# An RMS-normalised matrix product: B's first tile and A's second tile come in fp32 by the two hardware queues, and the preparation of A's row blocks is placed anew

## The chip, the core and the metric

The kernel runs on one core of a Trainium2 chip. Its five engines work side by side, each through its own instructions in order: TensorE (PE; PEld is its weight load), VectorE (DVE), ScalarE (ACT), GpSimd (POOL) and SyncE (SP). Three of them also issue DMA transfers: POOL through a software queue that can change the type on the way, SP and ACT through one hardware queue each, which can't. The metric is the device time of one execution in microseconds; for the kernel before it is the median of three runs.

## What is computed

```python
m, k, n = 2048, 2048, 2048            # a, b, gamma in fp32, eps = 1e-5
x = np.matmul(a, b)
rms = np.sqrt(np.mean(x ** 2, axis=-1, keepdims=True) + eps)
return (gamma * x / rms).astype(np.float32)
```

## The kernel before

**Tiles.** A has 16 blocks of 128 rows; K is cut into 16 tiles of 128 (KT), taken in pairs (KP = 8, the loop variable `kp`). B is kept whole in bf16 in `raw[j][kp]`: two halves `j` of 1024 columns, eight pairs of K tiles, two tiles `t` in each. A matmul is 128x128 by 128x512. The eight PSUM banks are `tbank` and `acc[0]` to `acc[6]`. Order is the order of the program text on each engine (`manual_schedule`).

**The head** (blocks 0 to 3 of A, left half of B; lines 450 to 468). A's first pair of K tiles comes in fp32 by the SP and ACT hardware queues into `a0f` (line 106). Everything else comes by POOL's software queue, cast to bf16: in order B pair 0 (two transfers, line 115), A pair 1 (line 119), B pair 1, A pair 2, B pair 2 and so on, with at most eight transfers in flight. PE first runs eight matmuls on zeros (`busy(8)`), then `transpose_first` turns A's first pair (eight fp32 transposes; DVE and ACT copy the result to `head_at`, line 179), then four more on zeros (`busy(4)`). Then for each `kp` `stream` does 14 matmuls into seven banks (line 409), and within them, after the number of matmuls that its last argument gives, `transpose_head(kp + 1)` turns the next pair of A (line 185) through `tbank`, which DVE copies to `head_at` (line 190). `stream_in_parts` does the eighth group in `tbank` (line 438). At `kp` 0 the transposes stand after 12 matmuls.

**The right half of the head** (`stream_right`, lines 476 to 513) streams B's right half as it lands: rows 0 and 1 plainly (four banks), rows 2 and 3 as one step of Strassen's scheme in Winograd's form (seven products of half size instead of eight; `product`, line 361). DVE makes the sums of B's quarters (`b_diff`, `b_rest`) and of A's (`a_sums`).

**Lines 519 to 634** end that scheme for rows 2 and 3 (`product` 6, 3, 5, 4 and `pair_ends`), evict the banks, and ready blocks 4 and 5: ACT's squares give a row norm (`row_norm`), DVE scales the rows to fp16 (`row_factor`, `row_apply`), PE turns them (`transpose_half`, line 198). `first_segment` is the first half-group (blocks 4 and 5, left half).

**Segments** (lines 642 to 763). Groups g = 2 to 7 are pairs of blocks, each with two halves; every half is one segment of Strassen products, and pairs of groups share a second step (`step`, line 400, in `block_segment` and `last_group`). Each later block is loaded by POOL (`load_block`), then `row_norm` on ACT, then `prepare` (line 248): DVE scales it to fp16 in two halves (`a16_half` and the block's own place) and SP turns each half with a DMA transpose (line 253) into `at(mb)`. `finish` (line 309) multiplies finished rows by the inverse root and gamma on DVE and stores them by SP's queue (line 317); an `x` slot is written again only when its store has landed. `last_group` and what follows it is the tail.

Of the kernel before, what the change touches and what calls it, by code (L numbers as in the profile page):

```python
# [17 lines left out]
def kernel(  # L18
# [14 lines left out]
    P = 128  # L33
# [74 lines left out]

    def ah(kp):
        return ah_slot[(kp - 1) % NAH]  # L110

    def load_b(j, kp):
        for t in range(2):
            lo = kp * W2 + t * P
            nc.gpsimd.dma_start(out=raw[j][kp][:, t, :],  # L115
                                in_=b[lo:lo + P, j * HALF:(j + 1) * HALF])

    def load_head(kp):
        nc.gpsimd.dma_start(  # L119
            out=ah(kp),  # L120
            in_=a[0:HB * P, kp * W2:(kp + 1) * W2].rearrange("(r p) k -> p r k", p=P))
        load_b(0, kp)
# [47 lines left out]
    def transpose_first():  # L170
        bank = [tbank, acc[6]]
        view = [b.rearrange("p (r m) -> p r m", r=HB) for b in bank]
        for t in range(2):
            for r in range(HB):
                nc.tensor.matmul(view[t][:, r, :], a0f[:, r, t * P:(t + 1) * P], identity_f,
                                 is_transpose=True, start=(r == 0), stop=(r == HB - 1))
        for t, copy in enumerate((nc.vector.tensor_copy, nc.scalar.copy)):
            for h in range(2):
                copy(out=head_at[:, t, 2 * h:2 * h + 2, :], in_=view[t][:, 2 * h:2 * h + 2, :])

# [67 lines left out]
    def prepare(mb):  # L248
        row_factor(mb)
        src, f = a32.pop(mb), factor.pop(mb)  # L250
        for h, dst in enumerate((a16_half, src.bitcast(FP16)[:, 0:HALF])):
            nc.vector.tensor_scalar_mul(out=dst, in0=src[:, h * HALF:(h + 1) * HALF], scalar1=f)
            nc.sync.dma_start_transpose(at(mb)[:, h * KP:(h + 1) * KP, :], dst)
# [197 lines left out]
    busy(4)  # L451
    for kp in range(KP):
# [7 lines left out]
        stream(kp, before, len(groups1) + {0: 5, 1: 3}.get(kp, 2))  # L460
# [15 lines left out]
    def stream_right(kp):  # L476
# [11 lines left out]
        if kp == KP - 1:  # L488
            product_matmul(PAIR, 1, 7, p7, kp - 1, True)
        product_matmul(PAIR, 1, 2, u4, kp, True)  # L490
# [4 lines left out]

    for kp in range(KP):
# [22 lines left out]
    r2, r3 = HB - 2, HB - 1  # L519
    x11, x12, x21, x22 = (x_chunk(r, c) for r in (r2, r3) for c in (2, 3))  # L520
    copy_on("A")(out=x11, in_=u2)
# [6 lines left out]
    product(PAIR, 1, 6, u2, start=False)  # L528
# [5 lines left out]
    row_apply(HB + 1)  # L534
    evict(plain[2:3], "A")
    product(PAIR, 1, 3, acc[0])
    product(PAIR, 1, 5, u4, start=False)
    turned = [transpose_half(HB, h, (tbank, acc[1])[h]) for h in range(2)]
    take_transposed(HB, 0, turned[0], nc.scalar.copy)
    take_transposed(HB, 1, turned[1], nc.vector.tensor_copy)  # L540
    load_block(HB + 3)
    for r in range(HB):
        take_pre(r)
    square_right(0)
    evict(plain[3:], "A")
    square_right(1)

    def turn(h):
        view = transpose_half(HB + 1, h, (tbank, acc[2])[h])
        take_transposed(HB + 1, h, view, nc.vector.tensor_copy)  # L550

    for kp in range(KP):
        if kp == 6:
            turn(0)
        product_matmul(PAIR, 1, 4, u2, kp, False)
    turn(1)
    load_block(HB + 4)
    a_sums(G0, (3, 1, 2), False)

    def pair_ends():  # L560
        nc.scalar.copy(out=x22, in_=p7)
        nc.scalar.copy(out=x12, in_=u4)
        add(x21, u2, x22)
        add(x22, x12, x22)
        add(x12, acc[0], x12)

# [44 lines left out]
    def first_segment():  # L611
        n, g, j = 0, G0, 0
        nxt = 2 * g + 2
        do(n, 1)
        do(n, 7, False)
        finish(0, (1,))
        pair_ends()
        do(n, 2)
        row_norm(nxt)
        a_sums(g, (4,))  # L620
        finish(0, (0,))
        do(n, 6)
        do(n + 1, 1)
        prepare(nxt)
# [17 lines left out]
    def segment(n):  # L642
# [8 lines left out]
        own = nxt + (g == NG - 2)  # L651
# [7 lines left out]
        if j == 0:  # L659
            square_right(ra - 2)  # L660
            prepare(own)
            a_sums(g, (4,))
            finish(ra - 2, (0, 1) if g < NG - 2 else (0,))
# [19 lines left out]
        if j == 1 and g + 2 < NG:  # L683
            wait_for(at(nxt + 1)[:, KT - 1, 0:1])
            if G0 < g < NG - 3:
# [8 lines left out]
        if j == 0 and g < NG - 2:  # L694
            row_norm(nxt + 1)
        if j == 1:
            a_sums(g + 1, (3,))
            if g == NG - 3:
# [3 lines left out]
        if j == 0 and g == NG - 2:  # L702
# [7 lines left out]
        if j == 0:  # L710
            square_half(rb, 0)
            if g < NG - 2:
# [3 lines left out]
        else:  # L716
            if g == NG - 3:
                prepare(nxt + 2)
# [5 lines left out]
    def block_segment(n):  # L724
# [6 lines left out]
        row_norm(nxt)  # L731
        do(n - 1, 3)
        step(g - 1, 2, W2)
        step(g - 1, 6, X2)
# [3 lines left out]
        prepare(nxt)  # L738
# [9 lines left out]
        row_norm(nxt + 1)  # L748
        add(x10, W2, x10)
        add(x11, W2, x11)  # L750
        take_pre(ra - 2)
        do(n, 7)
        add(x10, X2, x10)
        a_sums(g, (4,))
        prepare(nxt + 1)
# [156 lines left out]
```

## Time and profile before

| | |
|---|---|
| time, median of 3 runs | 219.94 us (218.92 to 220.41) |
| the profiled execution: its time, its span | 218.97 us, 217.2 us |
| mean granted TensorE clock | 0.995 |
| DVE, ACT, POOL busy | 161.4, 113.1, 35.6 us |
| read from HBM, written | 34.60 MB, 16.78 MB |

The span runs from the first to the last instruction; 1.77 us of the execution's time lie outside it. Times in the views are microseconds from the span's start. In a timeline a row is one or more like instructions: start, time taken, engine, line, operation, out<-in, count; square brackets give the idle time before it and what ended it. A matmul's time is modelled with its drain, so neighbours overlap: 128x512 matmuls start 0.216 us apart (16.07 to 19.96, one turn of the head, holds sixteen of them and eight transposes that take 0.45), and the page shows 379 ns for one.

### The profile page before, as it was taken

What the parts mean: (1) busy time and instruction counts of PE and PEld (TensorE: products, weight loads), DVE (VectorE), ACT (ScalarE), POOL (GpSimd) and SP (SyncE); (2) the same over time, 40 slices, a digit from 0 to 9 for tenths busy, and PEclk for the clock granted to TensorE, in tenths of its full rate; (3) what the DMA queues carried; (4) which work ended last, traced back from release to release, by engine and by line L of the source; (5) the groups of instructions that cost most, each with busy time, mean ns of one, the idle gap of its engine ahead of it and who ended that gap; (6) DMA issues with size and microseconds to landing.
All of it is one profiled execution on the core that took longest, in us unless ns stands there. A gap on an engine that the chain in (4) does not pass through costs nothing.

```text
span 217.2 us, 2953 instructions
## 1 busy us (share of the span) xinstructions
PE 207.3 (95%) x1000; PEld 97.2 (45%) x1020; DVE 161.4 (74%) x323; ACT 113.1 (52%) x222; POOL 35.6 (16%) x74
## 2 busy tenths in 40 slices
PE   7999999999999999999999999999999999999960
PEld 3544544444455444444444444444444444444420
DVE  1128869999899997788975899399859883385771
ACT  2110002900599569498626962585777651555771
POOL 7554444334001000100021001102010000000020
PEclk9999999999999999999999999999999999999997
DMA  7999999999959798978674975499985960040455
GB/s 152 168 202 210 201 204 210 212 206 213 405 202 382 290 263 229 330 295 241 162 239 172 340 246 96 187 237 271 278 307 153 284 218 0 0 193 3 193 191 195
DMA packets 37040, 46.60 MB, mean 215 GB/s; under 512 B 22561, under 2 KB 26657, under 8 KB 35745
## 3 DMA queue, kind: packets, MB, share of 16 engines
q0 software_dynamic: 10608, 23.86, 44.8%
q1 hardware_dynamic: 26144, 22.29, 33.9%
q10 hardware_dynamic: 272, 0.26, 0.3%
q8 instruction: 8, 0.13, 0.2%
q14 instruction: 8, 0.06, 0.1%
HBM read 34.60 MB, written 16.78 MB: 237 GB/s over the span
## 4 chain that ended last, share of the span: by engine, by line
PE 68%; DMA 23%; DVE 2%; POOL 2%; issue 2%; ACT 1%; ACTq 0%; DVEq 0%; POOLq 0%
PE acc L361 61%; DMA b<-in_b_dram 18%; DMA early<-in_a_dram 5%; PE acc L400 3%; PE tbank L400 2%; POOL b L115 1%; DVE early L101 1%; PE tbank L361 1%; POOL early L119 1%; ACT a L779 1%; PE acc L198 0%; PE tbank L198 0%; DVE acc L529 0%; DVE x L101 0%; DVE b L101 0%
## 5 line engine op out<-in xcount | busy, mean ns | idle before, releaser
L361 PEld LDWEIGHTS <-s 128*128 128x128 f16 (+1 forms) x312 | 30.5, 98 | 36.9 <-DVE s L338 0.3
L275 ACT ACTIVATE sq<-x 128x1024 bf16<-128x1024 f32 (+1 forms) x33 | 33.2, 1005 | 22.6 <-DVE x L101 18.8
L409 PE MATMUL acc<-b,head_at 128*128 128x512 bf16 x171 | 42.1, 379 | 0.2
L314 DVE SCALAR_TENSOR_TENSOR x<-x,r,gamma_sb 128x1024 f32<-128x1024 f32 x28 | 35.0, 1282 | 0.5
L361 PE MATMUL acc<-b,head_at 128*128 128x512 bf16 x135 | 33.9, 379 | 0.2
L101 DVE TENSOR_TENSOR x<-acc,x 128x512 f32<-128x512 f32 x33 | 22.2, 686 | 12.5 <-PE acc L361 6.7
L361 PEld LDWEIGHTS <-head_at 128*128 128x128 f16 (+1 forms) x192 | 18.7, 98 | 22.2
L361 PE MATMUL acc<-b,at_even 128*128 128x512 bf16 x110 | 26.2, 379 | 0.1
L361 PE MATMUL acc<-early,s 128*128 128x512 bf16 x100 | 25.3, 379 | 0.2
L409 PEld LDWEIGHTS <-head_at 128*128 128x128 bf16 x176 | 16.9, 98 | 19.1
L361 PE MATMUL acc<-b,s 128*128 128x512 bf16 x102 | 24.1, 379 | 0.2
L227 ACT ACTIVATE sq<-a 128x1024 bf16<-128x1024 f32 x22 | 23.3, 1058 | 1.7 <-DMA a<-in_a_dram 1.4
L361 PEld LDWEIGHTS <-at_even 128*128 128x128 f16 x160 | 15.6, 98 | 18.6
L361 PE MATMUL acc<-t_left,s 128*128 128x512 bf16 x93 | 22.2, 379 | 0.1
L115 POOL DMA_DIRECT2D b<-in_b_dram x32 | 17.2, 540 | 20.5 <-DMA b<-in_b_dram 13.8
L448 ACT COPY x<-acc 128x512 f32<-128x512 f32 x7 | 4.0, 581 | 25.3 <-PE acc L409 25.3
L591 ACT COPY acc<-acc 128x512 f32<-128x512 f32 x12 | 6.9, 575 | 10.4 <-PE acc L361 10.4
L190 DVE COPY head_at<-tbank 128x1024 bf16<-128x1024 bf16 x7 | 4.8, 693 | 7.5 <-PE tbank L185 7.5
L296 DVE RECIPROCAL r<-rms 128x1 f32<-128x1 f32 x16 | 2.5, 159 | 9.7 <-ACT rms L291 9.7
L101 DVE TENSOR_TENSOR x<-tbank,x 128x512 f32<-128x512 f32 x9 | 6.2, 690 | 4.2 <-PE tbank L438 4.1
L782 POOL TENSOR_SCALAR x<-x,r 128x512 f32<-128x512 f32 x2 | 1.4, 688 | 47.8 <-DVE r L296 47.8
L593 ACT COPY x<-acc 128x512 f32<-128x512 f32 x10 | 5.8, 584 | 5.3 <-PE acc L361 4.9
(129 smaller groups left out, 243.4 us busy)
## 6 DMA issues: line engine op xcount, KB each, us to landing
out_dram<-x SPq DMA_DIRECT2D x29, 512.0 KB, 3.0
a<-in_a_dram POOLq DMA_DIRECT2D x9, 1024.0 KB, 6.0
b<-in_b_dram POOLq DMA_DIRECT2D x32, 256.0 KB, 9.9
a<-in_a_dram POOLq DMA_DIRECT2D x4, 512.0 KB, 9.8
early<-in_a_dram POOLq DMA_DIRECT2D x7, 256.0 KB, 10.0
gamma_sb<-in_gamma_dram POOLq DMA_DIRECT2D x2, 512.0 KB, 9.8
head_at<-in_a_dram POOLq DMA_DIRECT2D x1, 1024.0 KB, 7.8
out_dram<-x SPq DMA_DIRECT2D x3, 256.0 KB, 2.6
```

What stands on the lines that cost most here:

```text
L101: nc.vector.tensor_tensor(out=out, in0=in0, in1=in1, op=op)
L115: nc.gpsimd.dma_start(out=raw[j][kp][:, t, :], in_=b[lo:lo + P, j * HALF:(j + 1) * HALF])
L190: nc.vector.tensor_copy(out=head_at[:, 2 * kp:2 * kp + 2, :, :], in_=view)
L227: nc.scalar.activation(out=junk, in_=a32[mb][:, h * HALF:(h + 1) * HALF], func=ACTF.Square, scale=2.0 ** -8, accum_out=n2[:, h:h + 1])
L275: nc.scalar.activation(out=sq[:, 0:src.shape[-1]], in_=src, func=ACTF.Square, scale=inv_sqrt_n, accum_out=msq[mb][:, c:c + 1])
L314: nc.vector.scalar_tensor_tensor(out=x, in0=x, scalar=inverse_of[mb], in1=gamma_sb[:, h * HALF:(h + 1) * HALF], op0=ALU.mult, op1=ALU.mult)
L361: nc.tensor.matmul(bank, lhsT[:, kp, :], rhs, start=(start and kp == 0), stop=(kp == KP - 1), skip_group_check=not start)
L400: nc.tensor.matmul(bank, lhsT[:, k, :], rhs, start=(m in (1, 7) and k == 0), stop=(k == KQ - 1), skip_group_check=m not in (1, 7))
L409: nc.tensor.matmul(bank, head_at[:, kt, r, :], head_rhs(c, kt), start=(kt == 0), stop=(kt == KT - 1))
L448: copy_on(engine)(out=x_chunk(*g), in_=banks[g])
L591: nc.scalar.copy(out=b3, in_=b2)
L593: nc.scalar.copy(out=chunks(n)[2], in_=B7)
```

## The change

A's second pair and the first tile of B pair 0 leave POOL's software queue: SP and ACT each issue, behind their half of A's first pair, half of that B tile (into the free slot `x_slot[5]`) and half of A's second pair (into `x_slot[4]`), in fp32. DVE and ACT cast them to bf16 in `transpose_first`. The zero matmuls after it go from four to two, and the transposes of pair 1 come after seven matmuls instead of twelve. In `stream_right`'s last turn four matmuls of product 6 come before product 2 (the copy to `x11` moves with them). Product 4 is done in three parts, with block 4's transposes, the first product of the first segment and block 5's transposes between them; product 7 of that segment comes after its product 2; `pair_ends` adds in another order. In the first segment `prepare` stands ahead of the second `finish`. From g = 3 on blocks 10 to 13 are prepared earlier than before (with the DMA transposes of block 12 held back by `turn=False` until `turn_half`), so that each segment has one block to prepare, with the loads and `finish` calls moved to suit.

```diff
@@ -106,19 +106,28 @@
         queue.dma_start(out=a0f[:, 2 * h:2 * h + 2, :],
                         in_=a[2 * h * P:(2 * h + 2) * P, 0:W2].rearrange("(r p) k -> p r k", p=P))
 
+    b0f = x_slot[HB + 1]
+    for h, queue in enumerate((nc.sync, nc.scalar)):
+        queue.dma_start(out=b0f[:, h * CH:(h + 1) * CH], in_=b[0:P, h * CH:(h + 1) * CH])
+    a1f = x_slot[HB].rearrange("p (r k) -> p r k", r=HB)
+    for h, queue in enumerate((nc.sync, nc.scalar)):
+        queue.dma_start(out=a1f[:, 2 * h:2 * h + 2, :],
+                        in_=a[2 * h * P:(2 * h + 2) * P, W2:2 * W2].rearrange("(r p) k -> p r k", p=P))
+
     def ah(kp):
         return ah_slot[(kp - 1) % NAH]
 
     def load_b(j, kp):
-        for t in range(2):
+        for t in range(1 if (j, kp) == (0, 0) else 0, 2):
             lo = kp * W2 + t * P
             nc.gpsimd.dma_start(out=raw[j][kp][:, t, :],
                                 in_=b[lo:lo + P, j * HALF:(j + 1) * HALF])
 
     def load_head(kp):
-        nc.gpsimd.dma_start(
-            out=ah(kp),
-            in_=a[0:HB * P, kp * W2:(kp + 1) * W2].rearrange("(r p) k -> p r k", p=P))
+        if kp > 1:
+            nc.gpsimd.dma_start(
+                out=ah(kp),
+                in_=a[0:HB * P, kp * W2:(kp + 1) * W2].rearrange("(r p) k -> p r k", p=P))
         load_b(0, kp)
 
     a32 = {}
@@ -174,9 +183,13 @@
             for r in range(HB):
                 nc.tensor.matmul(view[t][:, r, :], a0f[:, r, t * P:(t + 1) * P], identity_f,
                                  is_transpose=True, start=(r == 0), stop=(r == HB - 1))
+        for h, copy in enumerate((nc.vector.tensor_copy, nc.scalar.copy)):
+            copy(out=raw[0][0][:, 0, h * CH:(h + 1) * CH], in_=b0f[:, h * CH:(h + 1) * CH])
         for t, copy in enumerate((nc.vector.tensor_copy, nc.scalar.copy)):
             for h in range(2):
                 copy(out=head_at[:, t, 2 * h:2 * h + 2, :], in_=view[t][:, 2 * h:2 * h + 2, :])
+        nc.vector.tensor_copy(out=ah(1)[:, 0:2, :], in_=a1f[:, 0:2, :])
+        nc.scalar.copy(out=ah(1)[:, 2:4, :], in_=a1f[:, 2:4, :])
 
     def transpose_head(kp):
         view = tbank.bitcast(BF16).rearrange("p (t r m) -> p t r m", t=2, r=HB)
@@ -245,12 +258,19 @@
         a16[mb] = a16_slot[mb]
         nc.vector.tensor_scalar_mul(out=a16[mb], in0=a32.pop(mb), scalar1=factor.pop(mb))
 
-    def prepare(mb):
+    to_turn = {}
+
+    def prepare(mb, turn=True):
         row_factor(mb)
         src, f = a32.pop(mb), factor.pop(mb)
-        for h, dst in enumerate((a16_half, src.bitcast(FP16)[:, 0:HALF])):
+        to_turn[mb] = a16_half, src.bitcast(FP16)[:, 0:HALF]
+        for h, dst in enumerate(to_turn[mb]):
             nc.vector.tensor_scalar_mul(out=dst, in0=src[:, h * HALF:(h + 1) * HALF], scalar1=f)
-            nc.sync.dma_start_transpose(at(mb)[:, h * KP:(h + 1) * KP, :], dst)
+            if turn:
+                turn_half(mb, h)
+
+    def turn_half(mb, h):
+        nc.sync.dma_start_transpose(at(mb)[:, h * KP:(h + 1) * KP, :], to_turn[mb][h])
 
     x_half = {}
     slot_of = {(r, h): r + HB * h for r in range(HB) for h in range(2)}
@@ -448,7 +468,7 @@
             copy_on(engine)(out=x_chunk(*g), in_=banks[g])
 
     transpose_first()
-    busy(4)
+    busy(2)
     for kp in range(KP):
         if kp + 4 < KP:
             load_head(kp + 4)
@@ -457,7 +477,7 @@
         before = [lambda: transpose_head(kp + 1)] if kp + 1 < KP else []
         if kp == KP - 2:
             before.append(lambda: a_sums(PAIR, (3,), False))
-        stream(kp, before, len(groups1) + {0: 5, 1: 3}.get(kp, 2))
+        stream(kp, before, len(groups1) + {0: 0, 1: 3}.get(kp, 2))
         if kp == KP - 1:
             evict(groups1, "ADADADA")
         stream_in_parts(last1, kp)
@@ -486,13 +506,18 @@
         for g, kt in first:
             head_matmul(banks[g], *g, kt)
         if kp == KP - 1:
+            copy_on("A")(out=x11, in_=u2)
             product_matmul(PAIR, 1, 7, p7, kp - 1, True)
+            for k in range(4):
+                product_matmul(PAIR, 1, 6, u2, k, False)
         product_matmul(PAIR, 1, 2, u4, kp, True)
         if kp < KP - 1:
             product_matmul(PAIR, 1, 7, p7, kp - 1, True)
         for g, kt in second:
             head_matmul(banks[g], *g, kt)
 
+    r2, r3 = HB - 2, HB - 1
+    x11, x12, x21, x22 = (x_chunk(r, c) for r in (r2, r3) for c in (2, 3))
     for kp in range(KP):
         load_later(1)
         b_diff(1, kp)
@@ -516,53 +541,50 @@
 
 
 
-    r2, r3 = HB - 2, HB - 1
-    x11, x12, x21, x22 = (x_chunk(r, c) for r in (r2, r3) for c in (2, 3))
-    copy_on("A")(out=x11, in_=u2)
     product_matmul(PAIR, 1, 7, p7, KP - 1, True)
     b_rest(1, KP - 1)
     add(x11, u4, x11)
     evict(plain[:1], "A")
     row_norm(HB)
     row_norm(HB + 1)
-    product(PAIR, 1, 6, u2, start=False)
+    for kp in range(4, KP):
+        product_matmul(PAIR, 1, 6, u2, kp, False)
     nc.vector.tensor_copy(out=u4, in_=u2)
     row_factor(HB)
     row_apply(HB)
     evict(plain[1:2], "D")
     row_factor(HB + 1)
-    row_apply(HB + 1)
     evict(plain[2:3], "A")
     product(PAIR, 1, 3, acc[0])
     product(PAIR, 1, 5, u4, start=False)
+
+    def product_4(lo, hi):
+        for kp in range(lo, hi):
+            product_matmul(PAIR, 1, 4, u2, kp, False)
+
+    product_4(0, 2)
     turned = [transpose_half(HB, h, (tbank, acc[1])[h]) for h in range(2)]
     take_transposed(HB, 0, turned[0], nc.scalar.copy)
     take_transposed(HB, 1, turned[1], nc.vector.tensor_copy)
+    row_apply(HB + 1)
     load_block(HB + 3)
     for r in range(HB):
         take_pre(r)
+    evict(plain[3:], "A")
     square_right(0)
-    evict(plain[3:], "A")
-    square_right(1)
-
-    def turn(h):
-        view = transpose_half(HB + 1, h, (tbank, acc[2])[h])
-        take_transposed(HB + 1, h, view, nc.vector.tensor_copy)
-
-    for kp in range(KP):
-        if kp == 6:
-            turn(0)
-        product_matmul(PAIR, 1, 4, u2, kp, False)
-    turn(1)
-    load_block(HB + 4)
-    a_sums(G0, (3, 1, 2), False)
+    product_4(2, 6)
+
+    def turn_next():
+        for h in range(2):
+            view = transpose_half(HB + 1, h, (tbank, acc[2])[h])
+            take_transposed(HB + 1, h, view, nc.vector.tensor_copy)
 
     def pair_ends():
-        nc.scalar.copy(out=x22, in_=p7)
+        nc.scalar.copy(out=x21, in_=p7)
         nc.scalar.copy(out=x12, in_=u4)
-        add(x21, u2, x22)
-        add(x22, x12, x22)
+        add(x22, x12, x21)
         add(x12, acc[0], x12)
+        add(x21, u2, x21)
 
 
 
@@ -612,16 +634,21 @@
         n, g, j = 0, G0, 0
         nxt = 2 * g + 2
         do(n, 1)
+        square_right(1)
+        turn_next()
+        product_4(6, KP)
+        load_block(HB + 4)
+        a_sums(g, (3, 1, 2), False)
+        do(n, 2)
         do(n, 7, False)
+        pair_ends()
         finish(0, (1,))
-        pair_ends()
-        do(n, 2)
         row_norm(nxt)
         a_sums(g, (4,))
+        prepare(nxt)
         finish(0, (0,))
         do(n, 6)
         do(n + 1, 1)
-        prepare(nxt)
         do(n, 5)
         nc.scalar.copy(out=chunks(n)[2], in_=B7)
         take(n, 22)
@@ -648,7 +675,7 @@
             return
         first = g >= G2 and (g - G2) % 2 == 0
         do(n, 6)
-        own = nxt + (g == NG - 2)
+        own = nxt + (g >= G2)
         if j == 0:
             finish(ra - 1)
             row_norm(own)
@@ -659,8 +686,10 @@
         if j == 0:
             square_right(ra - 2)
             prepare(own)
+            if g == G2 - 1:
+                load_after(at(nxt)[:, KT - 1, 0:1], nxt + 2)
             a_sums(g, (4,))
-            finish(ra - 2, (0, 1) if g < NG - 2 else (0,))
+            finish(ra - 2, (0, 1) if g < G2 else (0,))
         else:
             if not first:
                 square_half(ra, 0)
@@ -682,7 +711,7 @@
         do(n + 1, 1)
         if j == 1 and g + 2 < NG:
             wait_for(at(nxt + 1)[:, KT - 1, 0:1])
-            if G0 < g < NG - 3:
+            if g in (G2,):
                 load_block(nxt + 2)
                 wait_for(a32[nxt + 2][:, 0:1])
             load_block(nxt + 3)
@@ -691,15 +720,15 @@
                 a_two_sums(g)
             a_sums(g + 1, (1, 2))
         do(n, 7)
-        if j == 0 and g < NG - 2:
+        if j == 0 and g < G2:
             row_norm(nxt + 1)
         if j == 1:
             a_sums(g + 1, (3,))
-            if g == NG - 3:
+            if G0 < g < NG - 2:
                 row_norm(nxt + 2)
         do(n, 5)
         take(n, 22)
-        if j == 0 and g == NG - 2:
+        if j == 0 and g >= G2:
             finish(ra - 2, (1,))
         if j == 1:
             take_pre(rb)
@@ -709,13 +738,13 @@
         take(n, 21)
         if j == 0:
             square_half(rb, 0)
-            if g < NG - 2:
+            if g < G2:
                 prepare(nxt + 1)
             if g == G2:
                 b_two(2)
         else:
-            if g == NG - 3:
-                prepare(nxt + 2)
+            if G0 < g < NG - 2:
+                prepare(nxt + 2, g != G2)
             if not first:
                 square_right(rb)
             if g == G0:
@@ -728,14 +757,15 @@
         do(n, 6)
         step(g - 1, 1, X2)
         nc.scalar.copy(out=W2, in_=X2)
-        row_norm(nxt)
+        row_norm(nxt + 1)
         do(n - 1, 3)
         step(g - 1, 2, W2)
+        for h in range(2):
+            turn_half(nxt, h)
         step(g - 1, 6, X2)
         nc.scalar.copy(out=Y2, in_=X2)
         square_right(ra - 1)
         add(x00, W2, x00)
-        prepare(nxt)
         load_after(at(nxt)[:, KT - 1, 0:1], nxt + 2)
         do(n + 1, 1)
         take(n - 1, 12)
@@ -745,14 +775,13 @@
         step(g - 1, 7, W2)
         step(g - 1, 4, X2)
         add(x11, Y2, x11)
-        row_norm(nxt + 1)
         add(x10, W2, x10)
         add(x11, W2, x11)
         take_pre(ra - 2)
+        prepare(nxt + 1)
         do(n, 7)
         add(x10, X2, x10)
         a_sums(g, (4,))
-        prepare(nxt + 1)
         step(g - 1, 3, Y2)
         do(n, 5)
         take(n, 22)
```

## The prediction

> **What bounds the kernel now.** First the page's busy times and slices, for whether one engine decides.
>
> ```profile
> PE 207.3 (95%) x1000; PEld 97.2 (45%) x1020; DVE 161.4 (74%) x323; ACT 113.1 (52%) x222; POOL 35.6 (16%) x74
> ...
> PE   7999999999999999999999999999999999999960
> ```
>
> PE is full from the second slice to the last but one. Next the waits of PE, because a full slice can hide short ones:
>
> ```profile
> PE acc L164 <- DVE pace L155: 1.5, 1, 1.5
> PE tbank L438 <- DVE head_at L190: 0.3, 1, 0.3
> ```
>
> That is the whole list. After 12.01 us PE waits for nobody until its last matmul at 210.2. So whatever the change moves behind the head can only lose time, and a gain must come from the first 12 us or the 7 us behind 210.2, which it leaves as they are. The timeline of PE at the start shows what there is to win:
>
> ```profile
> 4.84 1.06 PE L175 MATMUL tbank<-t_left,early 128*128 128x128 f32 x4
> 5.70 1.06 PE L175 MATMUL acc<-t_left,early 128*128 128x128 f32 x4
> 6.55 1.09 PE L164 MATMUL acc<-sq 128*128 128x512 bf16 x4
> 7.48 2.75 PE L409 MATMUL acc<-b,head_at 128*128 128x512 bf16 x12
> 10.18 0.62 PE L185 MATMUL tbank<-identity,early 128*128 128x128 bf16 x8
> 10.64 0.59 PE L409 MATMUL acc<-b,head_at 128*128 128x512 bf16 x2
> 11.58 0.59 PE L438 MATMUL tbank<-b,head_at 128*128 128x512 bf16 x2 [0.35 <-DVE head_at L190]
> 12.01 2.32 PE L409 MATMUL acc<-b,head_at 128*128 128x512 bf16 x9
> ```
>
> Four zero matmuls from 6.55 take 4 x 0.216 = 0.86 us. From 7.48 the first turn has 16 matmuls and eight transposes, 16 x 0.216 + 0.45 = 3.91 us, but the second begins at 12.01: 0.62 lost, mostly in the 0.94 from 10.64 to 11.58, where two matmuls (0.43) stand before a copy on DVE. The second turn takes 4.06 to 16.07 (0.15 lost, waiting for A's pair 2), the third 3.89. In all 0.86 + 0.62 + 0.15 = 1.63 us.
>
> Last, which transfers feed this. The DMA view of the first issues, and of two stretches by queue (q1 is SP's, q10 ACT's, q0 POOL's):
>
> ```profile
> early<-in_a_dram ACTq DMA_DIRECT2D x1, 256.0 KB, 3.8
> early<-in_a_dram SPq DMA_DIRECT2D x1, 256.0 KB, 3.5
> b<-in_b_dram POOLq DMA_DIRECT2D x1, 256.0 KB, 5.0
> ```
>
> ```profile
> DMA packets 178, 0.17 MB, mean 342 GB/s; under 512 B 11, under 2 KB 178, under 8 KB 178
> ```
>
> ```profile
> q0 software_dynamic: 80, 0.16, 96.5%
> q10 hardware_dynamic: 93, 0.08, 23.0%
> q1 hardware_dynamic: 15, 0.01, 3.2%
> ```
>
> ```profile
> q0 software_dynamic: 112, 0.20, 102.4%
> ```
>
> A's first pair (issued 0.73) lands at about 4.5, B's first tile (issued 1.24) at 6.24. The second fence is 3.0 to 3.5: the hardware queues alone move 0.17 MB in half a microsecond. The third, 3.5 to 4.5, has the software queue beside their last 0.09 MB. The fourth, 5.0 to 7.0, is that queue alone: 0.20 MB in 2 us, against 205 GB/s from 16 us on. POOL's resumed issues tell of the landings after that: A's pair 1 just before 10.42, where POOL's wait on it ends, and from then one transfer every 1.3 us.
>
> **The change part by part.** *Zero matmuls:* two fewer, 0.43, won only where B and `head_at` are ready: PE's earliest first product is 6.55 + 0.43 = 6.98.
>
> *B's tile and A's second pair on the hardware queues.* Behind A's first pair stand 0.52 MB of B and 0.52 MB of A. Their rate has not been seen beside a running software queue, so by rows: from above 0.17 MB in 0.5 us = 0.34 MB/us, from below what the tail got in the third fence, 0.09 MB in about 0.6 us (it was landed by 4.5) = 0.14. I take the middle, 0.24, since in 5 to 7 us the software queue used half of what it moves later and leaves room. From 3.6, with 0.09 MB of A still to move: B at 3.6 + 0.61/0.24 = 6.1, A's second pair 2.2 later at 8.3, each plus 0.4 from the last packet to the landing (as A's first pair shows, 4.1 to 4.54): 6.5 and 8.7. At the ends: 5.8 and 7.3, or 8.4 and 12.1.
>
> *Casts.* Not in the trace from fp32 in SBUF to bf16 at 128x512. DVE's nearest row is line 252, 128x1024 fp32 to fp16 in 0.74 us, so 0.37 to 0.74; half is the nearer, with half the elements. ACT's nearest is line 448, 128x512 in 0.58. On DVE the cast of B stands ahead of the two copies to `head_at` (0.76 for both): whoever waits for B holds them, and all of PE. So the first product is at 6.5 + 0.05 + 0.37 + 0.38 + 0.05 = 7.35, against 7.48. The second matmul needs ACT's half, 6.5 + 0.05 + 0.58 + 0.05 = 7.2: ready. Seven matmuls end at 8.86. The last six transposes need ACT's half of A: 8.7 + 0.05 + 0.58 + 0.05 = 9.4, so they end at 9.4 + 6 x 0.056 = 9.7; seven matmuls to 11.2, two more to 11.65. DVE's copy (0.69, from 9.8 to 10.5) is now beside the seven matmuls, which removes today's stall; what is late next is ACT's cast of A. Second turn at 11.65 instead of 12.01: -0.36. The software queue has two transfers fewer ahead of A's pair 2, so the 0.15 there goes too: -0.51. Best ends: 6.98 + 16 x 0.216 + 0.45 = 10.89, -1.12 - 0.15 = -1.27. Worst: A at 12.1, transposes to 13.1, second turn at 15.05, +3.0 - 0.15 = +2.9.
>
> *The software stream.* A gain at 12 us is kept only if the later tiles come earlier too: POOL waits for a landing every 1.3 us, three a turn, and PE's turn is 3.9; the last tile of B lands at 56.3 (DVE's wait for it ends at 56.38) and PE reads it at 56.72, 0.4 spare. Two transfers fewer are 2 x 1.27 = 2.5 us off the stream; the hardware queues' extra 1.04 MB costs 1.04/0.34 = 3.1 us of the same engines, less what the slack 2 us from 5 to 7 gives, about 1. Sum -0.4, so the stream keeps pace.
>
> The Trainium skill speaks against this: "DMA: Bandwidth & Descriptors", section "Rules for kernel authors", says that spreading transfers over SP, ACT and GpSimd does not help bandwidth, since all run on the same 16 engines and interleave. By the rule alone the stream would end 3.1 - 2.5 = 0.6 later and the gain would be eaten at 56 us; the row of 5 to 7 us is why I do not take it whole.
>
> *stream_right's end:* four matmuls move ahead of product 2, nothing is added, and B's last tile is needed 0.86 later (spare 1.3). The eviction of `acc[0]` and ACT's row norms behind it come 0.86 later: the second norm ends at 63.9 instead of 63.0.
>
> *Lines 519 to 634:* the order on PE changes, not its work. Walking ACT and DVE with their rows: `row_apply(4)` ends 63.4 (transposes at 63.63, covered), ACT's copy of `tbank` 64.4 to 65.4 (1.01), DVE's copy of `acc[1]` 64.8 to 65.5; the first product wants both at 65.4: +0.14. Block 5's transposes end at 68.2, so `a_sums` starts at 69.2 instead of 67.6, and DVE is 1.3 to 1.5 us behind up to 85. The sum s3 is ready at 69.9, needed at 70.3 since product 2 now covers it; today it is 68.3 against 68.43.
>
> *first_segment:* with `prepare` first, the store of `x_slot[0]` stands behind two DMA transposes on SP (1.27 each): issued at 79.4 instead of 75.11, landed 2.6 later at 82.0, where ACT's copy (line 599; 79.08 today) waits with all of ACT behind it. It frees `acc[1]` for the product at 84.1: 1.4 spare. Block 7's second transpose lands 1.2 later at 88.4, its sum s2 is ready at 89.9, needed at 91.0: 1.1 spare. Nothing.
>
> *Blocks 10 to 13 earlier:* ACT's squares of block 10 and 12 (2.6 each) fall into its idle 3.65 before 116.04 and 4.65 before 137.75; DVE's 2.3 for each into 1.60 before 117.55 (0.7 left, pushing a `finish` nobody waits for within 8 us) and 3.63 before 141.15. PE reads block 10 from 128.9, landed 126.7 today and earlier then. POOL's loads get less to wait for. SP's deferred transposes of block 12 follow a product that ends at 141, now 143.5. Nothing.
>
> Sum: -0.51 + 0.14 = -0.4: 218.97 - 0.4 = 218.6 for the profiled execution. Its time is 0.97 under the median of 219.94; the same step from the median gives 219.5.
>
> **The rivals.** *The whole window closes:* rate 0.34, -1.27 + 0.14 = -1.1, 217.8 (median 218.8). For: 342 GB/s and the slack from 5 to 7. Against: three queues then share 16 engines.
>
> *A's second pair comes late (the other side):* PE is in order, so a landing after 8.3 (8.97 less ACT's 0.68) holds the transposes and all behind them one for one; from 9.1 on the change loses. At 0.14 MB/us it is +2.9 + 0.14, 222.0 (median 223.0); at 0.19, A's first pair's own mean (0.52 MB from 1.8 to 4.5), the landing is 10.0, +0.9 in all, 219.9 (median 220.8). It loses over 1% from a landing at 11.3. For: the third fence. Against: the first pair itself.
>
> *It does nothing that lasts:* the start moves, and at 56 us PE waits for B: +0.1, 219.1 (median 220.1). For: 0.4 spare. *A wait in the first segment* for the store at 82.0, if that takes 4.6 as the first one did (71.26 to 75.83): 84.0, and the product waits 0.6: +0.2 in all.
>
> **How the numbers follow.** Forecast 0.45; whole window 0.23; late A 0.18; nothing that lasts or the first segment 0.14. The range, 218.2 to 221.2, takes the whole window with half a microsecond of the runs' spread below, and late A up to a landing of 10.3. About 1% (2.2 us) is what a measurement of this kernel tells from no change. No case here wins that much (1.63 is all there is), only runs that spread could show it: 0.04. Slower by more: the later half of late A, and a stall unseen in the segments: 0.11. The same: 0.85.
>
> **What would show it.** Right: the first line-409 product (now line 429) at 7.0 to 7.6, the second turn at 11.3 to 12.0 with no wait on `head_at`, no wait of PE behind it over 0.3. Wrong: PE's waits naming DVE's or ACT's cast (lines 187 to 192) for over a microsecond, B's tile landing after 7.5 or A's after 10, PE waiting for B between 50 and 57, or for ACT's copies between 65 and 92.

## The result and the profile after

The changed kernel takes 224.07 us (223.46 to 225.95, six runs) against 219.09 us for the kernel before, run beside it (218.92 to 220.41): a ratio of 1.0235, interval 1.0205 to 1.0265. It is 2.35% slower. (The 219.94 given ahead was the median of the first three runs of the kernel before; with three more it is 219.09.) The profiled execution took 223.91 us with a span of 222.1 us, 4.9 us more than before, at a mean granted clock of 0.981 instead of 0.995. First the busy times, the slices and the clock by slices:

```profile
PE 208.0 (94%) x998; PEld 97.1 (44%) x1018; DVE 161.7 (73%) x325; ACT 114.0 (51%) x224; POOL 34.7 (16%) x72
...
PE   7579999999999999999999999999999999999960
...
PEclk9969999999999999999999999999999999999995
```

In the kernel before, the clock by slices was

```profile
PEclk9999999999999999999999999999999999999997
```

PE is as busy as before (208.0 against 207.3). What is new sits in slices two and three, that is from 5.6 to 16.7 us: PE is idle for a part of the second and third, and in the third its clock is 0.6. PE's waits, the whole list again:

```profile
PE tbank L198 <- DVE early L191: 3.6, 1, 3.6
PE acc L173 <- DVE pace L164: 1.5, 1, 1.5
PE acc L429 <- DVE head_at L190: 0.8, 1, 0.8
```

The wait of 3.6 is the transposes of A's second pair waiting for its cast. Behind it there is no wait of PE on this list. The timeline of PE in the head:

```profile
6.07 0.59 PE L173 MATMUL acc<-sq 128*128 128x512 bf16 x2
7.47 1.68 PE L429 MATMUL acc<-b,head_at 128*128 128x512 bf16 x7 [0.80 <-DVE head_at L190]
12.77 1.10 PE L198 MATMUL tbank<-identity,early 128*128 128x128 bf16 x8 [3.62 <-DVE early L191]
13.66 2.73 PE L429 MATMUL acc<-b,head_at 128*128 128x512 bf16 x7
16.23 0.59 PE L458 MATMUL tbank<-b,head_at 128*128 128x512 bf16 x2
16.66 2.32 PE L429 MATMUL acc<-b,head_at 128*128 128x512 bf16 x9
```

The first product comes at 7.47, as before, the second turn at 16.66 instead of 12.01: +4.65. The last matmul of the kernel starts 4.73 later than before, so the head holds all but 0.08 of the loss. (Those 0.08 are at 69.81, where the first product of `first_segment` starts 0.297 behind the matmul ahead of it instead of 0.216.) In the fourth row the first six matmuls, from 13.66 to 15.80, start 0.43 us apart by the trace, twice the 0.216 of the kernel before; from there on it is 0.216 again. The table of stretches shows why; its columns are the stretch, its length, the busy time of PE, PEld, DVE, ACT and POOL with counts, the granted clock, the DMA share and GB/s:

```profile
9.00:12.00 3.00, 0.15 (x1) 0.00 (x0) 0.00 (x0) 0.00 (x0) 1.00 (x6) 1.00 1.15 244
12.00:14.00 2.00, 1.23 (x9) 0.90 (x10) 0.62 (x2) 0.62 (x1) 1.02 (x2) 0.59 1.32 206
14.00:16.00 2.00, 2.00 (x6) 0.71 (x5) 0.60 (x1) 0.00 (x0) 0.71 (x2) 0.55 1.16 202
16.00:18.00 2.00, 2.00 (x11) 0.92 (x10) 0.00 (x0) 0.59 (x1) 1.10 (x2) 1.00 1.30 208
```

PE does nothing from 9.2 to 12.8, and the clock averages 0.59 and 0.55 over the two stretches from 12 to 16: what they lack, 0.82 and 0.90 us, is worth some 3.4 us at half clock. The chain of waits names the transfer behind it:

```profile
1.26 0.45 SPq L111
1.76 10.41 DMA x<-in_a_dram
12.19 0.54 DVE early L191
12.77 1.10 PE tbank L198 x8
```

SP issues its half of A's second pair at 1.76 and it lands 10.4 us later, at 12.17 (ACT's half at 12.35). B's tile, one place ahead in the same queues, had landed at 6.63 and 6.87. The queues between the two, 6.5 to 12:

```profile
q0 software_dynamic: 470, 0.70, 76.4%
q1 hardware_dynamic: 264, 0.25, 18.1%
q10 hardware_dynamic: 266, 0.26, 13.6%
```

A's 0.51 MB took the 5.5 us, 0.09 MB/us. The two hardware queues together sent 530 packets, the software queue 470, so neither waits for the other to end. But the hardware queues' packets are rows of 1 KB, and the software queue's take 76.4% of the engines' time.

At the full clock the second turn would have come at 12.77 + 0.45 + 7 x 0.216 + 0.43 = 15.16; it came at 16.66. So 3.5 us of the distance to the 11.65 that was forecast are the late transfer, and 1.5 us the clock.

### The profile page after: what moved, and what is told of

It is laid out like the page before. It is cut to its first block, busy times and chain, and to the rows that moved or that the text cites. A ratio compares the mean times of both kernels' runs of the same rounds, so it can differ in the third digit from the quotient of the medians.

```text
span 222.1 us, 2959 instructions
## 1 busy us (share of the span) xinstructions
PE 208.0 (94%) x998; PEld 97.1 (44%) x1018; DVE 161.7 (73%) x325; ACT 114.0 (51%) x224; POOL 34.7 (16%) x72
## 4 chain that ended last, share of the span: by engine, by line
PE 84%; DVE 5%; DMA 5%; issue 2%; ACT 1%; SPq 0%; ACTq 0%
PE acc L381 57%; PE acc L429 17%; DMA x<-in_a_dram 5%; PE acc L420 3%; PE tbank L420 2%; PE tbank L198 2%; DVE x L101 2%; PE tbank L458 2%; DVE x L334 1%; PE tbank L381 1%; DVE a L268 1%; DVE a_half L268 1%; ACT a L808 1%; PE tbank L211 0%; PE acc L211 0%
## 5 line engine op out<-in xcount | busy, mean ns | idle before, releaser
L429 PE MATMUL acc<-b,head_at 128*128 128x512 bf16 x171 | 43.4, 386 | 1.1 <-DVE head_at L190 0.8
L381 PE MATMUL acc<-b,head_at 128*128 128x512 bf16 x134 | 33.8, 379 | 0.2
L123 POOL DMA_DIRECT2D b<-in_b_dram x31 | 16.7, 541 | 21.7 <-DMA b<-in_b_dram 15.8
```

The lines of the kernel that those rows point to most:

```text
L123: nc.gpsimd.dma_start(out=raw[j][kp][:, t, :], in_=b[lo:lo + P, j * HALF:(j + 1) * HALF])
L381: nc.tensor.matmul(bank, lhsT[:, kp, :], rhs, start=(start and kp == 0), stop=(kp == KP - 1), skip_group_check=not start)
L429: nc.tensor.matmul(bank, head_at[:, kt, r, :], head_rhs(c, kt), start=(kt == 0), stop=(kt == KT - 1))
```

## The experiments

The theory after this profile: A's second pair is late because of its place, second in the hardware queues, where its short rows take turns with a software queue that has by then started; and the hole that this leaves in PE costs the clock as well. The rivals: the new order behind the head costs the time; or the fp32 path with its casts is slow as such; or the hardware queues are slow at any second transfer, whatever the software queue does.

**Each part alone.** The first kernel has the old head and the new order behind it. Against the changed kernel (the lines of `b0f` and `a1f` go too):

```diff
-        for t in range(1 if (j, kp) == (0, 0) else 0, 2):
+        for t in range(2):
-        if kp > 1:
-            nc.gpsimd.dma_start(
+        nc.gpsimd.dma_start(
...
-    busy(2)
+    busy(4)
-        stream(kp, before, len(groups1) + {0: 0, 1: 3}.get(kp, 2))
+        stream(kp, before, len(groups1) + {0: 5, 1: 3}.get(kp, 2))
```

> The head as it was before, everything behind it as changed. Theory (the whole loss is A's second pair landing at 12.2 to 12.4 us, the hole of 3.6 us that it leaves on PE, and the half clock after the hole): second turn of the head at 12.0 us, the later reorders cost 0.1 to 0.3 us, so the time is 219.2 to 219.5 where before is 219.1. Rival (the reorders behind the head take a share): 1 us or more over before.

The second has the new head and the old order. Against the kernel before it has the change's hunks from line 106 to the casts, and these:

```diff
-    busy(4)
+    busy(2)
...
-        stream(kp, before, len(groups1) + {0: 5, 1: 3}.get(kp, 2))
+        stream(kp, before, len(groups1) + {0: 0, 1: 3}.get(kp, 2))
```

> The head as changed, everything behind it as before. Theory: A's second pair lands at 12.0 to 12.5, the second turn begins at 16.4 to 16.9, the time is 4.4 to 5.0 us over before. Rival (the reorders take a share, or the old order behind the head hides some): under 3.5 us over before.

Measured: the new order alone 220.16 us, ratio 1.0029 (1.0010 to 1.0049); the new head alone 224.48, ratio 1.0234 (1.0205 to 1.0264), which is the whole change's 1.0235. In the head alone A's second pair lands at 11.87 and 12.55 and PE waits 3.4 and 0.5 for its casts. (Its profiled execution is the longest of its four: the clock stays at 0.50 from 12 to 18 us, and the second turn comes at 17.70, where 16.4 to 16.9 was expected.) So the loss is the head's. The order behind it is not quite free by itself: it came out over the 219.2 to 219.5 expected, and its profiled execution, at 220.59 one of its longest, has waits of PE in `block_segment` of 0.3 and 0.2 for ACT's and DVE's copies. (A third, of 0.5 for a pair of A at 25.6, stands ahead of everything that the new order moves.) By itself it costs 0.1 to 0.5%; on top of the new head it adds nothing that these runs tell.

**Each of the two transfers alone on the hardware queues,** both with the new order behind the head. B's tile alone: A's second pair goes back to POOL's queue, and its transposes behind twelve matmuls. Against the changed kernel:

```diff
-    a1f = x_slot[HB].rearrange("p (r k) -> p r k", r=HB)
-    for h, queue in enumerate((nc.sync, nc.scalar)):
-        queue.dma_start(out=a1f[:, 2 * h:2 * h + 2, :],
...
-        stream(kp, before, len(groups1) + {0: 0, 1: 3}.get(kp, 2))
+        stream(kp, before, len(groups1) + {0: 5, 1: 3}.get(kp, 2))
```

> B's first tile in fp32 by the hardware queues and cast, A's second pair by the software queue as before, turned after 12 matmuls as before, two zero matmuls. Theory (what hurts is a megabyte on the hardware queues beside the software stream, A's half of it last in line): B lands at 6.4 to 6.9 and the first product is at 7.3 to 7.6; A's pair, now the second software transfer, lands at 10 to 11; second turn 12.0 to 12.9, the time 0 to 1 us over before, the granted clock 0.99 or more. Rival (the casts in the way of the copies on DVE and ACT are what hurts): 2 us or more over before.

A's second pair alone: B's tile goes back to POOL's queue, and there are four zero matmuls again. Against the changed kernel:

```diff
-    b0f = x_slot[HB + 1]
-    for h, queue in enumerate((nc.sync, nc.scalar)):
-        queue.dma_start(out=b0f[:, h * CH:(h + 1) * CH], in_=b[0:P, h * CH:(h + 1) * CH])
...
-    busy(2)
+    busy(4)
```

> A's second pair in fp32 by the hardware queues right behind the first and cast, B's first tile by the software queue as before, four zero matmuls, the transposes after seven matmuls. Theory (place in line decides): A's rows land at 6.5 to 7.5, B's first software transfer later than the 6.2 of before, at 7.5 to 9; the first product waits for it, the second turn is at 11.5 to 13.5, the time within -0.5 to +1.5 us of before. Rival (A's rows of 1 KB are slow wherever they stand): they land after 9 and the time is 2 us or more over before.

Measured: B alone 219.65, ratio 1.0015 (1.0002 to 1.0028); it lands at 6.46 and 6.91, the first product comes at 7.52. A alone 219.15, ratio 0.9996 (0.9984 to 1.0009). A's second pair, now the first in line behind the first pair, lands at 5.69 and 6.02, and PE never waits for its cast; timeline of PE:

```profile
7.70 1.67 PE L424 MATMUL acc<-b,head_at 128*128 128x512 bf16 x7
9.21 0.61 PE L193 MATMUL tbank<-identity,early 128*128 128x128 bf16 x8
...
11.60 2.32 PE L424 MATMUL acc<-b,head_at 128*128 128x512 bf16 x10
```

The same transfer, of the same rows, in fp32, with the same casts, is there 6.4 us earlier; the second turn comes at 11.60. So neither the hardware queue nor the cast is slow as such: either transfer alone is early, and it is the second place that is late.

**The two in the other order.**

```diff
-    b0f = x_slot[HB + 1]
-    for h, queue in enumerate((nc.sync, nc.scalar)):
-        queue.dma_start(out=b0f[:, h * CH:(h + 1) * CH], in_=b[0:P, h * CH:(h + 1) * CH])
     a1f = x_slot[HB].rearrange("p (r k) -> p r k", r=HB)
...
+    b0f = x_slot[HB + 1]
+    for h, queue in enumerate((nc.sync, nc.scalar)):
+        queue.dma_start(out=b0f[:, h * CH:(h + 1) * CH], in_=b[0:P, h * CH:(h + 1) * CH])
```

> As changed, but A's second pair stands ahead of B's tile on both hardware queues. Theory (beside the software stream each queue gets its turn row by row, so A's 1 KB rows move half as fast as B's 2 KB rows, and whoever stands last pays): A lands at 5.7 to 6.5, B last in line at 9 to 10.5; first product at 10 to 11.5, second turn at 14 to 16 with the clock dropping in the hole before the first product, time 2 to 4 us over before. Rival (queues share by bytes): B lands as late as A did, 11.5 to 12.5, time 4 us or more over before.

Measured: 224.56, ratio 1.0246 (1.0214 to 1.0279). A lands at 5.75 and 6.12, and B, now second, at 10.02 and 10.20. PE's wait moves with it:

```profile
PE acc L429 <- DVE head_at L190: 4.4, 1, 4.4
```

The second in line is late whichever it is. B's rows are 2 KB and it is done 2.2 us sooner than A was in that place: from 6.5 to 9.5 the hardware queues moved 0.41 MB here and 0.30 MB in the changed kernel, with 225 and 295 packets against the software queue's 131 and 165. The ratio is nearly the same (1.7 and 1.8 to 1), which speaks for turns by packet, so that what a packet carries counts; the two matrices differ in more than their rows, so it is not shown by itself. B's landing met the expectation, the time did not: 5.5 over the kernel before, where 2 to 4 was expected, with the clock at 0.50 from 9 to 14 us and the second turn at 16.94.

**The hole filled.** Sixteen matmuls on zeros stand ahead of the transposes, so that PE isn't idle:

```diff
     def transpose_head(kp):
+        if kp == 1:
+            for _ in range(16):
+                nc.tensor.matmul(tbank, warm[:, 0:P], warm[:, 0:CH], start=True, stop=True)
```

> As changed, with 16 zero matmuls (3.46 us) in the hole between the first seven products and the transposes of A's second pair, so that PE works while it waits. Theory (the loss has two parts, a hole of 3.6 us and a half clock after it that costs about 1.5 us): A lands at 12.0 to 12.5, the second turn begins at 14.7 to 15.4, the granted clock stays at 0.99 or more, time 2.6 to 3.4 us over before. Rival (the clock has no part in it): second turn at 16.2 or later, 4.2 us or more over before.

Measured: A lands at 11.85 and 12.02, so 0.3 earlier than in the changed kernel, and the clock stays at 1.00 in every stretch of the head. Timeline of PE:

```profile
8.84 3.62 PE L197 MATMUL tbank<-sq 128*128 128x512 bf16 x16
12.36 0.87 PE L201 MATMUL tbank<-identity,early 128*128 128x128 bf16 x8
...
15.01 2.32 PE L432 MATMUL acc<-b,head_at 128*128 128x512 bf16 x10
```

The second turn comes at 15.01 as expected, 1.65 earlier than in the changed kernel, 0.3 to 0.4 of it by the earlier landing. So the clock's part is about 1.3, near the 1.5 worked out above. The time is 222.79, ratio 1.0175 (1.0148 to 1.0202): 3.7 over the kernel before, more than expected by 0.3. Behind the head, at 150.75 in `block_segment`, two matmuls start 0.62 apart instead of 0.216, for a sum on DVE.

**The transposes put back behind twelve matmuls,** everything else of the change kept:

```diff
-        stream(kp, before, len(groups1) + {0: 0, 1: 3}.get(kp, 2))
+        stream(kp, before, len(groups1) + {0: 5, 1: 3}.get(kp, 2))
```

> As changed, but the transposes of A's second pair stand after twelve matmuls, as before, instead of seven. Theory (the clock drops only after a hole of some length): the five matmuls shorten the hole to 2 to 2.5 us, the clock stays at 0.99 or more, the second turn begins at 14.0 to 14.8, time 2 to 2.9 us over before. Rival (a hole of 2 us drops it as well): second turn at 15.2 or later, time 3.4 us or more over before.

Measured: 222.97, ratio 1.0168 (1.0133 to 1.0204). The five matmuls that now lie in the hole wait 0.6 for B's second tile, which POOL's queue lands at 9.7; the hole shrinks to 1.59 and the second turn comes at 14.96. But the clock falls all the same, later; the table of stretches:

```profile
12.00:14.00 2.00, 1.22 (x10) 0.66 (x11) 0.94 (x2) 0.62 (x1) 1.28 (x2) 1.00 1.31 207
14.00:16.00 2.00, 1.77 (x5) 0.70 (x5) 0.18 (x1) 0.58 (x1) 0.57 (x2) 0.59 1.17 202
16.00:18.00 2.00, 2.00 (x7) 0.70 (x5) 0.00 (x0) 0.00 (x0) 1.24 (x2) 0.56 1.30 209
```

No wait of PE in the head is longer than 1.6 us here (1.45, 0.61, 1.59 and 0.35, from 5.8 to 14.2). The expectation, a full clock and 2 to 2.9 us over the kernel before, was missed: it is 3.9. (The profiled execution is the longest of four. One of the others took 221.86 us at a mean clock of 0.996, the rest have 0.984 to 0.986; so the clock may not fall in every execution of this kernel.)

**The software stream held back** until SP's half of A's second pair has landed, by a copy on POOL ahead of its second transfer. In the first version the copy wrote the tile `pace`, which DVE's and ACT's first work uses:

```diff
+    wait_for(a1f[:, 0, 0:1])
     for kp in range(1, 4):
         load_head(kp)
```

> As changed, but POOL issues its second and later transfers only when the first half of A's second pair has landed, so that the hardware queues share with one software transfer alone. Theory (sharing with the software stream is what makes A late): A lands at 7 to 8, the second turn begins at 11.2 to 12.2, time -0.3 to +0.8 us of before. Rival (a megabyte on the hardware queues takes that long by itself): A lands after 10, time 2.5 us or more over before.

The second version has a tile of its own:

```diff
+    held = consts.tile([P, 1], FP32, name="held")
+    nc.gpsimd.tensor_copy(out=held, in_=a1f[:, 0, 0:1])
     for kp in range(1, 4):
         load_head(kp)
```

> The changed kernel with POOL's second and later transfers held back until SP's half of A's second pair has landed, by a copy into a tile of its own, so that no other engine waits for that copy. Theory (A is late because its 1 KB rows take turns with the rows of the software queue): A's second pair lands at 9.5 to 9.9 instead of 12.2, the first product comes at 7.2 to 7.6, the transposes at 10.2 to 10.6 with a hole of PE of about 1.2 us and no clock lost; the loss is then put off to B's second pair, which POOL has asked for late and which lands at 14 to 17, so the third turn comes 2 to 3 us later than in the kernel before, and the time is 221 to 223. Rival (the hardware queues' second and third transfers are slow by themselves): A lands near 12 all the same.

Measured: 224.28, ratio 1.0242 (1.0216 to 1.0267), and 224.27, ratio 1.0232 (1.0214 to 1.0251). The first version held DVE's casts up until 9.9 (PE waits 3.3), so its time says little. In both, A's second pair lands at 9.6 to 9.8, 2.6 earlier than in the changed kernel: the software queue's packets are what it waits behind. From 7 to 9 us the hardware queues sent 418 packets in the second version and 213 in the changed kernel, beside 40 and 111 of the software queue. It was not the 7 to 8 first expected; the one software transfer already issued was still under way until 8.6 and 8.8, which may be why. In the second version the hole is the 1.2 expected, at full clock, but the transfers held back are then late; timeline of PE:

```profile
10.17 0.86 PE L200 MATMUL tbank<-identity,early 128*128 128x128 bf16 x8 [1.23 <-DVE early L193]
...
14.48 1.67 PE L431 MATMUL acc<-b,head_at 128*128 128x512 bf16 x7 [1.50 <-DMA b<-in_b_dram]
17.07 0.81 PE L431 MATMUL acc<-b,head_at 128*128 128x512 bf16 x3 [0.92 <-DMA b<-in_b_dram]
```

POOL's issue at 10.11 lands only at 14.44. The third turn comes at 20.28, 4.2 later than in the kernel before, where 2 to 3 was expected, and the time is over the 221 to 223 expected: the loss has only changed its name.

**Keeping what gained.** The kernel before, with only A's second pair on the hardware queues (and cast by DVE and ACT), and everything else old. Against the kernel before:

```diff
+    a1f = x_slot[HB].rearrange("p (r k) -> p r k", r=HB)
+    for h, queue in enumerate((nc.sync, nc.scalar)):
+        queue.dma_start(out=a1f[:, 2 * h:2 * h + 2, :],
...
-        stream(kp, before, len(groups1) + {0: 5, 1: 3}.get(kp, 2))
+        stream(kp, before, len(groups1) + {0: 0, 1: 3}.get(kp, 2))
```

> The kernel before with one thing taken from the change: A's second pair goes behind A's first on the two hardware queues in fp32 and is cast by DVE and ACT, its transposes after seven matmuls; both tiles of B's first pair stay on the software queue, the four zero matmuls stay, and everything behind the head is in the old order. Theory (what was late is the second thing in line on the hardware queues, not a transfer on them as such): A lands near 6.0, the first product comes at 7.5 to 7.8, the second turn at 11.5 to 11.7 instead of 12.01, and nothing behind gives it back, so 0.2 to 0.6 us less than before (ratio 0.997 to 0.999). Rival (the old order behind the head gives the start back when B's last tile is read near 56.7): a wait of PE for B between 50 and 57 and a ratio of 0.9995 to 1.001.

The same, with the transposes of the second turn after nine matmuls instead of ten:

```diff
-        stream(kp, before, len(groups1) + {0: 0, 1: 3}.get(kp, 2))
+        stream(kp, before, len(groups1) + {0: 0}.get(kp, 2))
```

> The same, with pair 2's transposes after nine matmuls of the second turn instead of ten. Theory (the 0.15 us lost in the second turn is the wait of the matmuls in tbank for DVE's copy of the transposes, and not for A's pair 2, as the prediction had it): the gap of 0.37 us before them goes, the third turn begins 3.91 us after the second instead of 4.06, and the time is 0.35 to 0.75 us under before. Rival (A's pair 2 is what is late there): the transposes wait for it instead and the second turn keeps its 4.06 us or more.

Measured: 219.19, ratio 1.0008 (0.9994 to 1.0022), and 219.15, ratio 1.0010 (0.9995 to 1.0025): no gain, where 0.2 to 0.75 us were expected, though the head did what it should. The second turn comes at 11.52 and 11.22 instead of 12.01. In the second kernel the third turn begins 3.90 after the second, so the 0.15 was DVE's copy, as the theory had it. But the last matmul starts only 0.18 earlier than before in both. Where the rest went is in the second kernel's waits of PE:

```profile
PE tbank L193 <- DMA early<-in_a_dram: 0.4, 1, 0.4
```

A's pair 4 lands at 21.14 and pair 5 at 25.56; in the kernel before they landed at 21.68 and 25.51. POOL's stream has one transfer fewer to carry. Its first B tile, 6.24 before, lands at 7.04 here, but A's pair 2, with the one transfer less ahead of it, at 13.06 instead of 13.98. That lead is gone by pair 5, while the hardware queues carry nothing; the queues from 7 to 25 us:

```profile
q0 software_dynamic: 3450, 3.50, 120.0%
q8 instruction: 1, 0.02, 0.3%
```

What took the lead is open. PE, in any case, catches up with the stream within four turns and stands at it. The rival had put this wait near 56.7; it came at 17 to 25. No kernel here beats the one before.

## Why the prediction was wrong

**The step that failed** is the rate in "B's tile and A's second pair on the hardware queues". The middle of 0.34 and 0.14, 0.24 MB/us, was taken for both transfers, "since in 5 to 7 us the software queue used half of what it moves later and leaves room". B's tile came near that: landed at 6.63 and 6.87, forecast 6.5. A's second pair got 0.09 MB/us, under the lower end, and landed at 12.17 and 12.35 instead of 8.7; the worst end of 12.1 was reached. The two met different neighbours. The queues from 3.5 to 5.0, POOL's in the kernel before and then all three in the changed kernel:

```profile
q0 software_dynamic: 126, 0.25, 104.4%
```

```profile
q1 hardware_dynamic: 120, 0.22, 70.9%
q10 hardware_dynamic: 131, 0.17, 31.4%
q0 software_dynamic: 1, 0.00, 0.9%
```

The software queue now starts at 5.0 instead of 3.5, which the prediction did not have (why is open), so that B's tile had more than half of its way to itself, and A's second pair had that queue beside it throughout. That B's forecast came out is thus partly luck, and one rate for both transfers was the mistake. Two readings behind it were wrong as well. The room was read from bytes; by the DMA share (the last column but one) the kernel before has little room from 5 to 6, and some from 6 to 7, beside the stream at its full rate:

```profile
5.00:6.00 1.00, 1.00 (x7) 1.00 (x6) 0.06 (x1) 0.00 (x0) 1.00 (x2) 1.00 1.21 102
6.00:7.00 1.00, 1.00 (x6) 0.74 (x5) 0.70 (x2) 0.20 (x1) 1.00 (x3) 1.00 0.83 95
...
16.00:20.00 4.00, 4.00 (x27) 2.04 (x25) 2.98 (x6) 0.00 (x0) 1.97 (x4) 1.00 1.25 205
```

And the lower end came from a stretch in which the software queue had just begun. The runs add what the bound lacked: behind a started software queue the second in line is late whichever it is, the more so with rows of 1 KB than of 2 KB (A second: 12.2; B second: 10.0), and 2.6 us earlier with that queue held.

**The late A** was a rival with the right mechanism: the hole, the place, one for one from 9.1. It was given 0.18, because A's first pair, alone on the engines, was taken as evidence against. Its price for a landing at 12.1, a second turn at 15.05, is borne out by the kernel with the hole filled (15.01, landed 11.85 and 12.02). What it lacked is the clock: 1.5 us by the spacing of the matmuls, 1.3 by that kernel. The Trainium skill has the rule ("TensorE: Matmul & The Clock Gate", Part 1): about 3.4 us without work return PE to half rate, and as much busy time brings the full rate back. The changed kernel's rows agree: a hole of 3.62, then some 3.4 us' worth of half clock. Others fit less well: in the head alone it lasts six us and more, and with the transposes after twelve matmuls the clock falls without such a hole.

**The zero matmuls and the casts** were right. DVE's cast of the B tile took 0.43 (0.37 forecast), ACT's 0.62 (0.58), the first product came at 7.47 (7.35).

**The 0.15 us in the second turn** was put down to waiting for A's pair 2. It was DVE's copy of the transposes: with pair 2 landed at 14.28 the turn still took 4.06 us in the changed kernel, and 3.90 once the transposes stood one matmul earlier.

**The software stream** was forecast 0.4 earlier; its last B tile landed at 57.09 instead of 56.29, 0.8 later. By the rule of the Trainium skill that the prediction cited against the change ("DMA: Bandwidth & Descriptors", "Rules for kernel authors") it would have been 0.6 later, which is nearer. But only part of the 0.8 can be put down to what the hardware queues carried: A's pair 2 lands 0.30 later (14.28 against 13.98) and pair 5 as well (25.81 against 25.51), and then the next B tile 1.23 later (28.00 against 26.77), long after the hardware queues' last packet at some 12 us. So that 0.6 comes close is in part luck. The two last kernels agree with the rule in what counts: a transfer moved off the software queue gave no gain that lasted, though there too the stream lost its lead where nothing shared the engines with it. With A on time, that is, "nothing that lasts" is what those kernels do.

**Behind the head** the forecast of +0.14 at the first product of `first_segment` became +0.08 there, and nothing else is on the list of PE's waits. That the block loads cost nothing is less sure: alone, the new order measured 0.1 to 0.5% over, with waits that the changed kernel doesn't show and of which the kernel with the hole filled has one.

**The sum.** The second turn was forecast at 11.65 and came at 16.66: +3.5 for the landing, +1.5 for the clock. The 0.15 didn't go. Less 0.06 at 69.81 that is +5.1, against 223.91 - 218.6 = 5.3. The rest is behind the last store: the span ended 1.0 us after it before and 1.2 after.

## What to carry to other kernels

Look at the DMA share and not at the GB/s alone before calling a stretch free, and price the second transfer in a line as if it met the other queue at full load, packet for packet. Where a change can open a hole in PE of some three microseconds, add the half clock behind it (here 1.3 to 1.5 us on top of 3.5, and more in the executions in which it lasts longer). And a gain at the start of a streaming stage is kept only if the stream itself comes earlier: 0.8 us won in the head were back to 0.18 once PE had caught up with the transfers.

## What was not expected of the hardware

The clock can fall without one long hole: with the transposes after twelve matmuls no wait was over 1.6 us, and the clock was 0.59 and 0.56 from 14 to 18 us. The Trainium skill has a case of this kind ("TensorE: Matmul & The Clock Gate", "A second HAM failure mode: psum-queue depth-cycling": frequent short idles between groups of matmuls make the clock swing). Yet the second kernel with the stream held back, with waits of 1.23, 1.50, 0.92 and 0.50, kept 1.00 from 8 to 20 us. What decides between the two stays open; it was not tried.

A software queue that has run dry is slow to come up to its rate. In the second kernel with the stream held back, POOL's issue at 10.11 had its first packet at 11.37 and landed at 14.44, while in a running stream landings follow each other by 1.3 us. The core's transfers ran at 34, 135, 107, 188 and 204 GB/s in the stretches of two us from 10 to 20.
